# First layer norm: statistics of the second token half from eviction row sums and ScalarE squares instead of VectorE's statistics instruction

## The chip, the core and the metric

The kernel runs on one core of one Trainium2 chip. The metric is the device time of one execution in microseconds (us), here as the median of three runs. TensorE (PE) multiplies matrices and writes to PSUM; VectorE (DVE) and ScalarE (ACT) do the elementwise work; GpSimd (POOL) helps a little; SyncE (SP) issues most of the loads.

## What is computed

The reference is a trunk of two layers on 256 tokens of width 2048: a Mamba-2 mixer and then a sliding-window attention mixer, each followed by a residual and a layer norm. The change touches the norm behind the first mixer.

```python
def _layernorm(x, g, b):
    mu = jnp.mean(xf, axis=-1, keepdims=True)
    var = jnp.mean(jnp.square(xf - mu), axis=-1, keepdims=True)
    y = (xf - mu) * lax.rsqrt(var + EPS) * g + b
    return y
...
    h = _mamba2_mixer(x, ...)            # ends in  y @ w_out   (4096 x 2048)
    x = _layernorm(ALPHA * x + h, ln_g[0], ln_b[0])
    k_sh, v_sh = _shared_kv(x, kv_w, kv_b, cos, sin)   # x @ kv_w  (2048 x 512)
    h = _swa_mixer(x, k_sh, v_sh, ...)
    x = _layernorm(ALPHA * x + h, ln_g[1], ln_b[1])
```

## The kernel before

**Products in three terms.** Every float32 product of a weight matrix is made of two parts per operand, a rounded high part H and the rest L. ScalarE writes the high part of each half (1024 columns) of a 128x2048 weight unit (L143, tile wh), VectorE the low part (L144, tile wl), and TensorE runs H·H, L·H and H·L as three matmuls per 128 rows of depth. All weights come from HBM in such units, in one long list (`srcs`); `next_unit` takes the next one and starts the load and split of a unit further on.

**Residual.** The stream x lies in xr as two token halves h = 0 and 1 of 128 tokens (the partitions) by 2048 columns. The output product of the mixer is added to it group by group. An `out_unit` is 12 matmuls (L330 to L332) into one PSUM bank for one token half and one block nb of 512 columns, and one VectorE instruction that evicts it. For the mixer that is L337: xr = psum * rms + xr, where rms is a scale per token.

**The last group and the norm.** `out_last` runs the last group's units in this order: half 0 block 0, half 1 block 0, half 0 blocks 1 to 3, then `done(0)`, then half 1 blocks 1 to 3, then `done(1)`. Behind each eviction `stats` is called, which is L823: VectorE's `bn_stats` over the 512 columns just written. `done1(h)` is the norm of one half: `bn_aggr` (L827) joins the four statistics into mean and variance, ScalarE makes rs = exp(-0.5 ln(var + eps)) in two instructions (L829, L830), and then for each block c of 512 columns VectorE runs t = (x - mean) * g (L845) and xr = t * rs + b (L848), TensorE turns the four 128x128 pieces (L853), ScalarE writes the high part x1H (L858) and VectorE the low part x1L (L859).

**What comes next.** The shared K/V product reads x1H and x1L, 128 columns of the width per matmul triple (L895 to L897), four triples per weight unit, first all of half 0 and then all of half 1. So block c of x1 feeds weight unit c. A second call of `out_last` at the end of the program serves the second norm (`done2`), with L339 as eviction and the same L823 and L827.

**Order.** Up to L812 (`order.close()`) the order of each engine's instructions is the written one. Behind it the order on each engine is chosen when the program is built, from what is expected to be ready; each engine then runs its own list in that order and waits where an input is late. In the trace, for example, weight halves of the K/V product (L144), which are written behind `done1`, stand between L823 and L827.

Of the kernel before, what the change touches and what calls it, by code (L numbers as in the profile page):

```python
# [8 lines left out]
F32 = mybir.dt.float32  # L9
F32R = mybir.dt.float32r  # L10
I32 = mybir.dt.int32
AF = mybir.ActivationFunctionType
ALU = mybir.AluOpType
AX = mybir.AxisListType

P = 128
S = 256
D = 2048
KT = D // P
NG = 8  # L20
# [42 lines left out]
def trunk(ctx: ExitStack, tc: tile.TileContext, A: dict, out: bass.AP, dbg=None):  # L63
    nc = tc.nc
    PSUM = bass.MemoryType.PSUM

    def pool(name, bufs=1, side=None, space=None, stack=ctx):
        kw = {"space": space} if space is not None else {}
        return stack.enter_context(
            tc.tile_pool(name=name, bufs=bufs, side=side, reuse_waits="tile", **kw)  # L70
        )
# [9 lines left out]
    def nm(s):  # L81
        uid[0] += 1
        return f"{s}_{uid[0]}"

    def mm_tile():
        return mm_ps.tile([P, 512], F32, tag="mm", name=nm("mm"), bufs=4)

    def ax_tile():
        return ax_ps.tile([P, 512], F32, tag="ax", name=nm("ax"), bufs=4)
# [9 lines left out]
    eps_t = cst.tile([P, 1], F32, tag="eps", name="eps_t")  # L99
# [162 lines left out]
    def next_unit():  # L262
        used[0] += 1
        fill_units()
        flush()
        return units[used[0] - 1]
# [29 lines left out]
    xr = xr_all[:, : 2 * D].rearrange("p (h d) -> p h d", h=2)  # L296
# [24 lines left out]

    xH = Split("xH", 1, 0, 192)
    xL = Split("xL", 1, 64, 192)
    def out_unit(aH, aL, h, u, nb, first, rms=None):

        ps = mm_tile()
        hs = slice(h * P, (h + 1) * P)
        for k in range(4):
            ks = slice(k * 512, (k + 1) * 512)
            nc.tensor.matmul(ps[:], aH[:, k, hs], u.h[:, ks], start=k == 0, stop=False)  # L330
            nc.tensor.matmul(ps[:], aL[:, k, hs], u.h[:, ks], start=False, stop=False)  # L331
            nc.tensor.matmul(ps[:], aH[:, k, hs], u.l[:, ks], start=False, stop=k == 3)  # L332
        v = xr[:, h, nb * 512 : (nb + 1) * 512]
        if first:
            nc.vector.scalar_tensor_tensor(v, v, ALPHA, ps[:], ALU.mult, ALU.add)
        elif rms is not None:
            nc.vector.scalar_tensor_tensor(v, ps[:], rms[:, h : h + 1], v, ALU.mult, ALU.add)  # L337
        else:
            nc.vector.tensor_tensor(v, v, ps[:], ALU.add)  # L339

    def out_last(aH, aL, rms, stats, done):

        us = []
        for nb in range(4):
            us.append(next_unit())
            out_unit(aH, aL, 0, us[nb], nb, False, rms)
            stats(0, nb)
            if nb == 0:
                out_unit(aH, aL, 1, us[nb], nb, False, rms)
                stats(1, nb)  # L350
        done(0)
        for nb in range(1, 4):
            out_unit(aH, aL, 1, us[nb], nb, False, rms)
            stats(1, nb)
        done(1)

# [155 lines left out]
    gs = [G() for _ in range(NG)]  # L512
# [256 lines left out]
    for g in range(NG):  # L769
        t = 10 * g  # L770
# [51 lines left out]
    def norm_stats(st, h, nb):  # L822
        nc.vector.bn_stats(st[:, h, nb, :], xr[:, h, nb * 512 : (nb + 1) * 512])  # L823

    def norm_scale(lp, st, h):
        mv = lp.tile([P, 2], F32, tag="mv", name=nm("mv"), bufs=2)
        nc.vector.bn_aggr(mv[:], st[:, h, :, :])  # L827
        rs = lp.tile([P, 1], F32, tag="rs", name=nm("rs"), bufs=2)
        nc.scalar.activation(rs[:], mv[:, 1:2], AF.Ln, bias=eps_t[:])  # L829
        nc.scalar.activation(rs[:], rs[:], AF.Exp, scale=-0.5)  # L830
        return mv, rs

    with ExitStack() as s2:
        lp = pool("lp", stack=s2)
        gb = lp.tile([P, 2, D], F32, tag="gb", name="gb1")
        nc.gpsimd.dma_start(gb[:, 0, :], A["lng"][0].partition_broadcast(P))
        nc.gpsimd.dma_start(gb[:, 1, :], A["lnb"][0].partition_broadcast(P))
        st1 = lp.tile([P, 2, 4, 6], F32, tag="st", name="st1")

        def done1(h):  # L840
            mv, rs = norm_scale(lp, st1, h)
            for c in range(4):
                sl = slice(c * 512, (c + 1) * 512)
                t = lp.tile([P, 512], F32, tag="t", name=nm("t"), bufs=2)
                nc.vector.scalar_tensor_tensor(  # L845
                    t[:], xr[:, h, sl], mv[:, 0:1], gb[:, 0, sl], ALU.subtract, ALU.mult
                )
                nc.vector.scalar_tensor_tensor(  # L848
                    xr[:, h, sl], t[:], rs[:], gb[:, 1, sl], ALU.mult, ALU.add
                )  # L850
                ps = ax_tile()
                for k in range(4):
                    nc.tensor.transpose(  # L853
                        ps[:, k * P : (k + 1) * P], xr[:, h, c * 512 + k * P : c * 512 + (k + 1) * P], ident
                    )
                dst = (slice(None), slice(c * 4, c * 4 + 4), slice(h * P, (h + 1) * P))
                psv = ps[:].rearrange("p (k t) -> p k t", k=4)
                nc.scalar.activation(x1H[dst], psv, AF.Copy)  # L858
                nc.vector.tensor_tensor(x1L[dst], psv, x1H[dst].bitcast(F32), ALU.subtract)  # L859

        if PRE:
            tc.keep_in_program_order(nc.scalar.preload_act_table_set("natural_log_exp_and_others"))
        out_last(*gs[NG - 1].y, gs[NG - 1].rms, lambda h, nb: norm_stats(st1, h, nb), done1)
    a_stack.close()


# [37 lines left out]
    for h in range(2):  # L904
        ps = mm_tile()
# [199 lines left out]
    for what, j in B_ORDER[:-1]:  # L1105
# [5 lines left out]
        else:  # L1111
            for nb in range(4):
                u = next_unit()
# [50 lines left out]
    if PRE:  # L1164
        tc.keep_in_program_order(nc.scalar.preload_act_table_set("natural_log_exp_and_others"))
    out_last(*os_[3], None, lambda h, nb: norm_stats(st2, h, nb), done2)


# [90 lines left out]
```

## Time and profile before

| | |
|---|---|
| median of 3 runs | 986.14 us (985.79 to 987.06) |
| the profiled execution | 987.56 us, its span 985.5 us |
| granted TensorE clock | 0.998 |
| VectorE busy | 796.8 us (81%) |
| ScalarE busy | 534.2 us (54%) |
| L823 (`bn_stats`, 128x512) | 16 times, 8 of them from 643.1 to 666.9 us and 8 at the end |

The span runs from the first to the last instruction that the profiler recorded; what lies around it is 2.06 us in the profiled execution. The chain of work that ended last names, at each moment, the instruction for which the end of the program had to wait. The timeline gives each instruction's start, its duration, and in brackets the idle time of its engine just before it with what ended it. Durations of neighbouring instructions overlap a little on DVE and ACT, so the pace of a row of them is read from start to start.

### The profile page before, as it was taken

How to read it: one execution, taken by the hardware profiler on the slowest of the kernel's cores; microseconds unless marked ns; L12 is line 12 of the kernel's file. 1: busy time of each engine (PE TensorE's matmuls, PEld its weight loads, DVE VectorE, ACT ScalarE, POOL GpSimd, SP SyncE). 2: the span in 40 equal slices, each digit the busy share in tenths (PEclk: the TensorE clock that was granted, in tenths of full speed). 3: DMA queues.
4: the chain of work that ended last, by engine and by line, in shares of the span. 5: the costliest groups of instructions: out<-in, count | busy, mean ns of one | idle time of the engine just before them, and what ended most of it. 6: DMA issues, size and time to landing. Idle time of an engine off the chain costs nothing.

```text
span 985.5 us, 17642 instructions
## 1 busy us (share of the span) xinstructions
PE 977.8 (99%) x6868; PEld 879.7 (89%) x6868; DVE 796.8 (81%) x1227; ACT 534.2 (54%) x905; POOL 167.9 (17%) x223
## 2 busy tenths in 40 slices
PE   9999999999999999999999999999999999999997
PEld 7999989999998998999999999887898888778975
DVE  6879897976987896796797698999657787888786
ACT  6586847455644834743744564444356464644632
POOL 0004004005046001200400400500212222130102
PEclk9999999999999999999999999999999999999999
DMA  9587885585586666668559657756774949493942
GB/s 357 187 273 275 271 286 160 189 311 161 172 288 200 206 232 209 196 200 302 152 176 307 183 175 240 238 174 189 224 249 122 339 140 341 153 310 123 328 155 86
DMA packets 69444, 218.72 MB, mean 222 GB/s; under 512 B 8097, under 2 KB 19633, under 8 KB 68593
## 3 DMA queue, kind: packets, MB, share of 16 engines
q1 hardware_dynamic: 63936, 201.05, 62.0%
q0 software_dynamic: 5136, 16.02, 5.0%
q8 instruction: 54, 0.88, 0.4%
q10 hardware_dynamic: 288, 0.52, 0.1%
q14 instruction: 30, 0.24, 0.1%
HBM read 205.37 MB, written 12.19 MB: 221 GB/s over the span
## 4 chain that ended last, share of the span: by engine, by line
PE 96%; DVE 2%; DMA 1%; ACT 0%; issue 0%; SPq 0%
PE mm L269 18%; PE mm L270 18%; PE mm L271 18%; PE mm L330 9%; PE mm L331 9%; PE mm L332 9%; PE mm L895 3%; PE mm L896 3%; PE mm L897 3%; PE ax L619 2%; PE ax L1079 1%; PE ax L1021 1%; DMA first<-in_first 1%; DVE st L823 0%; PE ax L539 0%; DVE t L1157 0%
## 5 line engine op out<-in xcount | busy, mean ns | idle before, releaser
L144 DVE TENSOR_TENSOR wl<-wr,wh 128x1024 fp32r<-128x1024 f32 (+2 forms) x338 | 397.9, 1207 | 76.0 <-ACT wh L143 75.1
L143 ACT ACTIVATE wh<-wr 128x1024 fp32r<-128x1024 f32 (+2 forms) x338 | 328.5, 1011 | 174.1 <-PE mm L331 79.4
L269 PE MATMUL mm<-xH,wh 128*128 128x256 f32 x1280 | 355.4, 278 | 0.3 <-ACT wh L168 0.3
L270 PE MATMUL mm<-xL,wh 128*128 128x256 f32 x1280 | 354.6, 277 | 0.0
L271 PE MATMUL mm<-xH,wl 128*128 128x256 f32 x1280 | 354.3, 277 | 0.0
L269 PEld LDWEIGHTS mm<-xH,wh 128*128 128x128 f32 x1280 | 240.4, 188 | 3.7 <-ACT wh L168 2.1
L270 PEld LDWEIGHTS mm<-xL,wh 128*128 128x128 f32 x1280 | 240.5, 188 | 1.2 <-DVE xL L164 0.2
L271 PEld LDWEIGHTS mm<-xH,wl 128*128 128x128 f32 x1280 | 240.3, 188 | 0.1
L636 POOL TENSOR_TENSOR yz<-yz,z 128x256 f32<-128x256 f32 x32 | 33.3, 1060 | 436.6 <-DMA wr<-in_wa 261.1
L330 PE MATMUL mm<-wh,yH 128*128 128x512 f32 x256 | 101.2, 395 | 0.0
L331 PE MATMUL mm<-wh,yL 128*128 128x512 f32 x256 | 99.9, 390 | 0.0
L332 PE MATMUL mm<-wl,yH 128*128 128x512 f32 x256 | 99.7, 389 | 0.0
L457 DVE SCALAR_TENSOR_TENSOR cv<-mm,pc,cv 128x255 f32<-128x255 f32 x144 | 69.1, 480 | 15.2 <-ACT cv L455 11.8
L270 PE MATMUL mm<-x1L,wh 128*128 128x256 f32 x256 | 70.8, 276 | 0.0
L269 PE MATMUL mm<-x1H,wh 128*128 128x256 f32 x256 | 70.7, 276 | 0.0
L271 PE MATMUL mm<-x1H,wl 128*128 128x256 f32 x256 | 70.7, 276 | 0.0
L895 PE MATMUL mm<-wh,x1H 128*128 128x512 f32 x160 | 63.7, 398 | 0.0
L897 PE MATMUL mm<-wl,x1H 128*128 128x512 f32 x160 | 62.6, 392 | 0.2 <-DVE wl L144 0.2
L896 PE MATMUL mm<-wh,x1L 128*128 128x512 f32 x160 | 62.6, 392 | 0.2 <-DVE x1L L859 0.2
L455 ACT ACTIVATE cv<-mm,pc 128x256 f32<-128x256 f32 x48 | 26.8, 558 | 64.0 <-PE mm L271 64.0
L330 PEld LDWEIGHTS mm<-wh,yH 128*128 128x128 f32 x256 | 48.1, 188 | 10.3 <-issue 1.2
L332 PEld LDWEIGHTS mm<-wl,yH 128*128 128x128 f32 x256 | 48.1, 188 | 10.2
(220 smaller groups left out, 1371.3 us busy)
## 6 DMA issues: line engine op xcount, KB each, us to landing
wr<-in_wa SPq DMA_DIRECT2D x154, 512.0 KB, 5.4
wr<-in_wo SPq DMA_DIRECT2D x64, 512.0 KB, 5.1
wr<-in_wq SPq DMA_DIRECT2D x32, 512.0 KB, 4.9
wr<-in_wg SPq DMA_DIRECT2D x32, 512.0 KB, 5.3
wr<-in_wb SPq DMA_DIRECT2D x32, 512.0 KB, 6.2
rb<-rscr SPq DMA_DIRECT2D x16, 512.0 KB, 8.0
el<-rscr SPq DMA_DIRECT2D x16, 256.0 KB, 7.3
wr<-in_wkv SPq DMA_DIRECT2D x8, 512.0 KB, 6.4
```

Source lines behind the costliest of these rows:

```text
L143: nc.scalar.activation(h[:, sl], raw, AF.Copy)
L144: nc.vector.tensor_tensor(l[:, sl], raw, h[:, sl].bitcast(F32), ALU.subtract)
L269: nc.tensor.matmul(ps, ah, bh, start=first, stop=False)
L270: nc.tensor.matmul(ps, ah, bl, start=False, stop=False)
L271: nc.tensor.matmul(ps, al, bh, start=False, stop=last)
L330: nc.tensor.matmul(ps[:], aH[:, k, hs], u.h[:, ks], start=k == 0, stop=False)
L331: nc.tensor.matmul(ps[:], aL[:, k, hs], u.h[:, ks], start=False, stop=False)
L332: nc.tensor.matmul(ps[:], aH[:, k, hs], u.l[:, ks], start=False, stop=k == 3)
L457: nc.vector.scalar_tensor_tensor(a[:, sft:], ps[:, : S - sft], w(3 - sft), a[:, sft:], ALU.mult, ALU.add)
L895: nc.tensor.matmul(ps[:], x1H[:, kk, hs], u.h[:, ks], start=kk == 0, stop=False)
L896: nc.tensor.matmul(ps[:], x1L[:, kk, hs], u.h[:, ks], start=False, stop=False)
L897: nc.tensor.matmul(ps[:], x1H[:, kk, hs], u.l[:, ks], start=False, stop=kk == KT - 1)
```

## The change

Half 0 keeps its statistics. For half 1 of the first norm the four `bn_stats` and the `bn_aggr` go. In their place:

- the four evictions of half 1 (L337) also write the sum of each row into `acc[:, nb]`;
- after block 0, ScalarE writes nm0 = -acc[:, 0] / 512, an estimate of minus the mean that is taken from the first 512 columns; after each block it runs one 128x512 `Square` of x + nm0 whose row sum goes to `sqs[:, nb]` (its elementwise output goes to a scratch tile sq);
- behind block 3 ScalarE runs seven small instructions (`scale_sums`): minus the mean, the mean of the squares, their correction for nm0, the variance, and Ln and Exp for the scale;
- `done1(1)` adds minus the mean (`nmu`) in L845 where it subtracted the mean, and takes the scale from `rs1`.

The second norm calls `out_last` without `total`, and with no rms, so its evictions (L339) and statistics are untouched.

```diff
-            nc.vector.scalar_tensor_tensor(v, ps[:], rms[:, h : h + 1], v, ALU.mult, ALU.add)
+            nc.vector.scalar_tensor_tensor(v, ps[:], rms[:, h : h + 1], v, ALU.mult, ALU.add, accum_out=total)
...
-                out_unit(aH, aL, 1, us[nb], nb, False, rms)
+                out_unit(aH, aL, 1, us[nb], nb, False, rms, total(nb))
...
+        sums = lp.tile([P, 16], F32, tag="sums", name="sums")
+        acc, sqs, (nm0, nmu, msq, d, d2, var, rs1) = (
+            sums[:, 0:4], sums[:, 4:8], [sums[:, i : i + 1] for i in range(8, 15)]
+        )
+
+        def stats1(h, nb):
+            if h == 0:
+                norm_stats(st1, h, nb)
+                return
+            if nb == 0:
+                nc.scalar.activation(nm0, acc[:, 0:1], AF.Copy, scale=-1.0 / 512.0)
+            sq = lp.tile([P, 512], F32, tag="sq", name=nm("sq"), bufs=1)
+            nc.scalar.activation(
+                sq[:], xr[:, 1, nb * 512 : (nb + 1) * 512], AF.Square, bias=nm0, accum_out=sqs[:, nb : nb + 1]
+            )
+
+        def scale_sums():
+            junk = lp.tile([P, 8], F32, tag="junk", name="junk")
+            nc.scalar.activation(junk[:, :4], acc, AF.Copy, scale=-1.0 / D, accum_out=nmu)
+            nc.scalar.activation(junk[:, 4:], sqs, AF.Copy, scale=1.0 / D, accum_out=msq)
+            nc.scalar.activation(d, nm0, AF.Identity, scale=-1.0, bias=nmu)
+            nc.scalar.activation(d2, d, AF.Square)
+            nc.scalar.activation(var, d2, AF.Identity, scale=-1.0, bias=msq)
+            nc.scalar.activation(rs1, var, AF.Ln, bias=eps_t[:])
+            nc.scalar.activation(rs1, rs1, AF.Exp, scale=-0.5)
+
         def done1(h):
-            mv, rs = norm_scale(lp, st1, h)
+            if h:
+                scale_sums()
+                shift, sop, rs = nmu, ALU.add, rs1
+            else:
+                mv, rs = norm_scale(lp, st1, h)
+                shift, sop = mv[:, 0:1], ALU.subtract
...
-                    t[:], xr[:, h, sl], mv[:, 0:1], gb[:, 0, sl], ALU.subtract, ALU.mult
+                    t[:], xr[:, h, sl], shift, gb[:, 0, sl], sop, ALU.mult
...
-        out_last(*gs[NG - 1].y, gs[NG - 1].rms, lambda h, nb: norm_stats(st1, h, nb), done1)
+        out_last(*gs[NG - 1].y, gs[NG - 1].rms, stats1, done1, lambda nb: acc[:, nb : nb + 1])
```

## What was predicted before the change was timed

> **What bounds the kernel now.** I read the page first: its span (985.5 us), the busy times, and the chain of work that ended last.
>
> ```profile
> PE 977.8 (99%) x6868; PEld 879.7 (89%) x6868; DVE 796.8 (81%) x1227; ACT 534.2 (54%) x905; POOL 167.9 (17%) x223
> ...
> PE 96%; DVE 2%; DMA 1%; ACT 0%; issue 0%; SPq 0%
> ```
>
> TensorE sets the end. The change takes nothing from TensorE, so it can only pay where TensorE waits. All that it can win lies in the 2% of the chain that is VectorE. So I asked for the chain of waits from 659 to 675 us, where the first norm is. Its columns are start, duration, and what ran.
>
> ```profile
> 659.48 0.69 DVE x1L L859
> ...
> 664.01 1.19 DVE st L823 x2
> 665.20 0.65 DVE xr L337
> 665.85 1.13 DVE wl L144
> 666.98 0.60 DVE st L823
> 667.59 1.12 DVE wl L144
> 668.71 0.17 DVE mv L827
> 668.88 1.08 DVE wl L144
> 669.96 0.72 DVE t L845 x2
> 671.20 0.76 DVE xr L848
> ...
> 673.39 0.70 DVE x1L L859
> ...
> 674.14 0.50 PE mm L896
> ```
>
> From 659.48 to 671.96 us the chain is VectorE's queue, one instruction behind the other: it is working off a backlog. Three statistics of half 1 stand in it (664.01 twice, 666.98) and the `bn_aggr` (668.71). At 674.14 us TensorE gets the first low part of half 1 and the chain is TensorE's again. How much TensorE lost there is read from its own timeline: start, duration, line, and in brackets its idle time.
>
> ```profile
> 666.48 0.39 PE L896 MATMUL mm<-wh,x1L 128*128 128x512 f32 x1
> 667.04 0.50 PE L897 MATMUL mm<-wl,x1H 128*128 128x512 f32 x1 [0.17 <-DVE wl L144]
> 667.38 0.39 PE L895 MATMUL mm<-wh,x1H 128*128 128x512 f32 x1
> ...
> 668.30 0.40 PE L896 MATMUL mm<-wh,x1L 128*128 128x512 f32 x1
> 668.76 0.50 PE L897 MATMUL mm<-wl,x1H 128*128 128x512 f32 x1
> ...
> 671.39 0.39 PE L896 MATMUL mm<-wh,x1L 128*128 128x512 f32 x1
> 672.09 1.29 PE L853 MATMUL ax<-cc,xr 128*128 128x128 f32 x8 [0.31 <-DVE xr L848]
> 673.41 0.51 PE L895 MATMUL mm<-wh,x1H 128*128 128x512 f32 x1
> 674.14 0.50 PE L896 MATMUL mm<-wh,x1L 128*128 128x512 f32 x1 [0.22 <-DVE x1L L859]
> ...
> 675.40 0.39 PE L895 MATMUL mm<-wh,x1H 128*128 128x512 f32 x1
> 675.63 0.60 PE L853 MATMUL ax<-cc,xr 128*128 128x128 f32 x4
> 675.98 0.49 PE L896 MATMUL mm<-wh,x1L 128*128 128x512 f32 x1
> ```
>
> The bracketed idle times understate the loss, since a matmul's recorded 0.39 us overlaps the next; starts tell more. In steady running the next matmul starts 0.23 us later (675.40 to 675.63), and four transposes take 0.35 us (675.63 to 675.98). Against that: 666.48 to 667.04 loses 0.33, and the step after it (0.34) another 0.11; 668.30 to 668.76 loses 0.23, and I put the same 0.11 behind it, 0.34 together; 671.39 to 672.09 loses 0.47; the eight transposes to 673.41 take 1.32 and not 0.70, so 0.62; 673.41 to 674.14 loses 0.50, with 0.10 behind it. Sum: 0.44 + 0.34 + 0.47 + 0.62 + 0.60 = about **2.4 us**. This is the ceiling in this stage, 0.25% of the time. The first two losses (0.78) are waits for a weight half (wl), the rest (1.7) waits for the norm of half 1; all have VectorE's backlog behind them.
>
> **What the change removes.** Half 1's four L823 and one L827. The first L823 of half 1 stands at about 643.7 us, in the pair that starts at 643.1, ahead of the backlog: its 0.6 us is worth nothing. In the backlog go 1.19 + 0.60 + 0.17 = **1.96 us** of VectorE's queue.
>
> **What it adds on VectorE.** Four evictions with a row sum, of which three (blocks 1 to 3) are in the backlog. No VectorE instruction with a row sum is in this trace. The nearest rows are ScalarE's exponentials with a row sum, where the sum is read out by an instruction of its own, and VectorE's smallest instructions.
>
> ```profile
> 860.19 0.19 ACT L1044 ACTIVATION_READ_ACCUMULATOR p<-p,sm 128x1 f32 x1
> 860.28 0.39 ACT L1044 ACTIVATE p<-p,sm 128x128 f32<-128x128 f32 x1
> ...
> L676 DVE SCALAR_TENSOR_TENSOR r<-r 128x2 f32<-128x2 f32 x24 | 3.9, 161 | 0.8
> L337 DVE SCALAR_TENSOR_TENSOR xr<-mm,r,xr 128x512 f32<-128x512 f32 x64 | 45.6, 742 | 3.5 <-PE mm L332 3.4
> L848 DVE SCALAR_TENSOR_TENSOR xr<-t,rs,gb 128x512 f32<-128x512 f32 x8 | 5.8, 743 | 0.0
> L548 DVE TENSOR_TENSOR e<-e,cbm 128x1536 f32<-128x1536 f32 x16 | 27.6, 1754 | 0.2
> L1049 DVE TENSOR_TENSOR p<-p,sm 128x1024 f32<-128x1024 f32 x8 | 9.7, 1215 | 0.0
> ```
>
> The read-out moves ScalarE's next start by 0.09 us (860.19 to 860.28). A VectorE instruction on two elements lasts 0.161. I take 0.10 per eviction, the nearest being the read-out itself: 3 x 0.10 = 0.30 us. Bounds: 0 (the sum is free) and 0.16 per eviction (0.48 together). A larger cost, a slower pass of the eviction itself, is a rival below. The page "Vector Engine (DVE) Microarchitecture Reference" of the Trainium skill speaks against the change here: § Points that are easy to get wrong says that this kind of instruction runs at half rate when both sources are wide SBUF tensors, as no port is left for the accumulator. This trace shows no such loss without a sum: L848, with both sources in SBUF, takes 743 ns and L337, with one in PSUM, 742 ns; with a sum no run here shows it yet. By that rule, were it to hold for the eviction too, the sum would be that of the fourth rival.
>
> Net on VectorE's queue: 1.96 - 0.30 = **1.66 us** less ahead of 674 us.
>
> **What it adds on ScalarE.** ScalarE was idle for 6 us in the stretch in question, up to 668.92.
>
> ```profile
> 632.92 1.28 ACT L862 ACT_TABLE_LOAD   x1
> ...
> 652.43 0.29 ACT L829 ACTIVATE rs<-mv,eps_t 128x1 f32<-128x1 f32 x1 [7.18 <-DVE mv L827]
> ...
> 661.70 1.21 ACT L858 ACTIVATE x1H<-ax 128x512 fp32r<-128x512 f32 x2
> 668.92 0.29 ACT L829 ACTIVATE rs<-mv,eps_t 128x1 f32<-128x1 f32 x1 [6.01 <-DVE mv L827]
> 669.24 0.20 ACT L830 ACTIVATE rs<-rs 128x1 f32<-128x1 f32 x1
> ...
> L1160 ACT ACTIVATE t<-t,rs 128x512 f32<-128x512 f32 x4 | 2.8, 721 | 1.3 <-DVE t L1157 1.3
> ```
>
> A `Square` of 512 columns with a pointer operand I price as L1160, 0.72 us, plus 0.10 for the read-out: 0.82. Those of blocks 1 and 2 can run from about 662.9 on, when the two L858 are done, into 6 us of idle time; they cost nothing. The one of block 0 and the nm0 copy run near 644 us, ahead of the 7.18 us of idle time before 652.43; nothing is queued behind them there but one weight cast.
>
> Block 3 starts the chain that matters. Its eviction moves from 665.20 to 665.20 - 1.19 + 0.20 = 664.2, and ends with its sum at about 664.95. Then Square, to 665.8. Then seven small instructions, each needing the one before or nearly so; a step takes 0.32 (668.92 to 669.24), two of them with 0.10 for a read-out: 7 x 0.32 + 0.20 = 2.44. So minus the mean is there at about 666.2 and the scale at **668.2 us**.
>
> Is that in time? In VectorE's queue L845 would come at 669.96 - 1.66 = 668.3 and the first L848 at 671.20 - 1.66 = 669.5. The chain is ready 1.3 us before L848 wants it, because the three weight halves (1.13 + 1.12 + 1.08) stand in front. If that cover were gone, L848 would wait, and the weight halves behind it. The new wait thus has a margin of 1.3 us against an estimated chain of 3.3 us. No DMA is issued, moved or passed by the change; the SP and POOL queues keep their lists.
>
> **What is late next.** With 1.66 us less, the first low part of half 1 (L859) starts at 671.7 and TensorE's L896 at 674.14 - 1.66 = 672.5. Without the two waits for weight halves TensorE reaches that point at 671.39 - 0.78 + 0.23 + 0.70 + 0.23, about 671.8. So 0.7 us of the stall is left, and TensorE is 1.66 us ahead of before. Does it keep this? Behind 690 us the waits of TensorE are a single row, at the very end:
>
> ```profile
> PE ax L1146 <- ACT dg L1136: 0.9, 1, 0.9
> ```
>
> Nothing is waited for in between, so weights and casts, which follow TensorE's consumption, have room for it to be 1.7 us earlier.
>
> **Sum.** Span 985.5 - 1.66 = 983.8; the profiled execution had 987.56 - 985.5 = 2.06 around it, so 985.9. The profiled one was 1.42 above the median shown, so as a median 986.14 - 1.66 = **984.5 us**. With both bounds of the read-out the gain is 1.5 to 2.0.
>
> **The rivals.**
>
> *The whole stall goes* (983.8). Behind L812 the order is chosen anew. If the weight halves fill the wait for ScalarE and the blocks of the norm go ahead of the third half, TensorE never starves and all 2.4 us are won. For it: the chain is ready by 668.2, and the remaining stall of 0.7 us is smaller than one weight half. Against it: VectorE has no gap to give, and the third half is itself needed by about 669.5. 983.4 to 984.1.
>
> *The norm waits a little for ScalarE* (985.4). The margin of 1.3 us goes if the new order assumes a shorter chain than the hardware needs, or puts Squares in front of the two L858. A table switch belongs here: the table load at 632.92 takes 1.28 us, and one in the chain would use up the margin. The Trainium skill's page "ScalarE: Activation LUTs", § Table sets: the hidden batching unit, says that cheap functions are in every set but does not name Square among its examples; no row before shows one. The gain is then 0.3 to 1.2 us.
>
> *The weight halves are held up* (987.6, slower). VectorE runs its list in order. If L845 and L848 of half 1 are put ahead of the first weight half, L845 stands waiting for ScalarE until 666.2, two L845 take it to 667.5, L848 waits until 668.2 and two of them take 1.4; then 1.13 for the weight half: 670.7. TensorE needs that half at 666.48 + 0.23 = 666.7, and so loses 4.0 us where it lost 2.4: 1.6 slower. If all four blocks go first (six more instructions of 0.66 in place of the two L848), it is 673.3 and 4.2 slower, 990.3. The point from which it decides: the first half must be done by 666.7 + 2.4 = 669.1. For it: the norm is written ahead of these loads. Against it: in the chain above a weight half stands in each gap between dependent steps (behind 665.20, 666.98 and 668.71), so such gaps have been filled.
>
> *The row sum doesn't relieve VectorE* (986.0). If an eviction with a sum streamed at half rate, it would cost as much as 512 more elements: 1754 - 1215 = 0.54 us (L548 against L1049). Three of them are 1.6 us, and the gain is gone. So it is, too, if the evictions wait for ScalarE's writes to the neighbouring columns of `sums`. Against the latter: TensorE reads the first half of a weight unit at 667.04 while VectorE writes the second from 667.59, so waits go by region.
>
> **How the numbers follow.** Forecast 0.44 (984.1 to 985.0), whole stall 0.25, small wait 0.16, held-up halves 0.09, no relief 0.06. The range takes in all but the held-up halves and the edges: 983.4 to 986.4. A measurement of this kernel can tell about 0.2%, or 2.0 us, from no change, so most of the forecast's cases count as the same: faster 0.28 (the whole stall, and the edge of the forecast), slower 0.07 (most of the held-up halves), same 0.65.
>
> **What will show it.** L823 falls from 16 to 12 and L827 from 4 to 3. The chain of waits near 665 us has no L823 and a short VectorE read-out; evictions stay at 0.74 us (else the fourth rival). ScalarE's scale is ready before VectorE's first L848 of half 1, with no bracketed wait on ScalarE there (else the second or third). TensorE's gap before the transposes of half 1 falls from 0.47 to near nothing, and the low part of half 1 comes about 1.7 us earlier. The prediction is wrong if TensorE waits longer for a wl than before, or if it gains here and new waits appear behind 690 us.

## The result, and the profile after

| | before | changed |
|---|---|---|
| median of 19 runs each, us | 986.76 (985.04 to 988.39) | 984.98 (983.31 to 985.66) |
| ratio of the two, 95% interval | | 0.998 [0.9974, 0.9987] |
| span of the profiled execution, us | 985.5 | 983.5 |

The changed kernel is 1.78 us faster by the medians. The interval of the ratio, times 986.76, makes that 1.3 to 2.6 us: a small gain, but not none. The forecast was a gain of 1.66 us.

Lines behind the change have new numbers: L845 is now L876, L848 is L879, the transposes L853 are L884, the high part L858 is L889, the low part L859 is L890, and the K/V matmuls L895 to L897 are L926 to L928. New are L850 (nm0), L852 (Square) and L858 to L864 (the seven small steps). First the page of the changed kernel, its busy times and the chain that ended last:

```profile
PE 976.9 (99%) x6868; PEld 880.0 (89%) x6868; DVE 794.3 (81%) x1226; ACT 538.8 (55%) x921; POOL 168.0 (17%) x223
...
PE 98%; DVE 1%; ACT 0%; issue 0%
```

VectorE gave up 2.5 us (796.8 to 794.3), ScalarE took on 4.6 (534.2 to 538.8), and TensorE's share of the chain rose from 96 to 98%. Of these two points only VectorE's (2% before, 1% now) is the change's; the other is the 1% of DMA in the chain before, one of the program's first loads (`first`). The groups of instructions by line, of the changed kernel (busy us and mean ns of one behind the first bar, idle time behind the second):

```profile
L337 DVE SCALAR_TENSOR_TENSOR xr<-mm,r,xr 128x512 f32<-128x512 f32 x64 | 45.6, 742 | 3.3 <-PE mm L332 3.2
L823 DVE BATCH_NORM_STATS2 st<-xr 128x6 f32<-128x512 f32 x12 | 8.3, 694 | 0.4
```

The statistics fell from 16 to 12, and the evictions stay at 742 ns. That is a mean of 64, of which four have a row sum; the three of these in the stage take 0.74 us each.

**Where in the program the gain lies.** The stage is measured from the first K/V matmul to the first transposed key, both on TensorE. Start, duration and line from TensorE's timeline, before and then changed:

```profile
659.81 0.39 PE L895 MATMUL mm<-wh,x1H 128*128 128x512 f32 x1
...
697.69 1.03 PE L922 MATMUL ax<-cc,kd 128*128 128x128 f32 x8
```

```profile
659.47 0.39 PE L926 MATMUL mm<-wh,x1H 128*128 128x512 f32 x1
...
696.00 1.03 PE L953 MATMUL ax<-cc,kd 128*128 128x128 f32 x8
```

The stretch fell from 37.88 to 36.53 us: 1.35 us of the 2.0 between the two spans. The rest is not the change's. The start at 659 us is 0.34 earlier already; 0.33 of that is there within the program's first 25 us. And about 900 us the unchanged kernel's profile loses 0.32 us among attention matmuls, which a kernel that keeps all statistics (the first experiment) doesn't lose either, though it gains nothing in this stage.

**How the stage runs now.** VectorE's timeline of the changed kernel, from the eviction of half 1's block 2 on:

```profile
661.74 0.74 DVE L337 SCALAR_TENSOR_TENSOR xr<-mm,r,xr 128x512 f32<-128x512 f32 x1
662.41 0.08 DVE L337 DVE_READ_ACCUMULATOR xr<-mm,r,xr 128x1 f32 x1
662.41 0.68 DVE L890 TENSOR_TENSOR x1L<-ax,x1H 128x512 fp32r<-128x512 f32 x1
663.01 0.74 DVE L337 SCALAR_TENSOR_TENSOR xr<-mm,r,xr 128x512 f32<-128x512 f32 x1
...
664.28 1.21 DVE L144 TENSOR_TENSOR wl<-wr,wh 128x1024 fp32r<-128x1024 f32 x1
665.41 1.40 DVE L876 SCALAR_TENSOR_TENSOR t<-xr,sums,gb 128x512 f32<-128x512 f32 x2
666.74 1.41 DVE L879 SCALAR_TENSOR_TENSOR xr<-t,sums,gb 128x512 f32<-128x512 f32 x2
...
668.96 1.32 DVE L890 TENSOR_TENSOR x1L<-ax,x1H 128x512 fp32r<-128x512 f32 x2 [0.15 <-ACT x1H L889]
...
671.52 1.22 DVE L144 TENSOR_TENSOR wl<-wr,wh 128x1024 fp32r<-128x1024 f32 x1
```

Two things are to be seen. The read-out of the row sum is recorded at the very moment at which the next instruction starts (662.41), so it takes no place in the queue: 0.67 us lie from an eviction's start to the next start. And the order is another. Before, three weight halves stood between the last eviction and the norm of half 1; now one does (664.28), and the second follows only at 671.52. So the first low part of half 1 starts at 668.96 where it started at 673.39: 4.4 us earlier (4.1 behind the stage's own start), not 1.7.

ScalarE's timeline of the changed kernel, behind the last eviction:

```profile
663.89 0.73 ACT L852 ACTIVATE sq<-xr,sums 128x512 f32<-128x512 f32 x1
...
664.61 0.19 ACT L858 ACTIVATE junk<-sums 128x4 f32<-128x4 f32 x1
664.99 0.28 ACT L860 ACTIVATE sums<-sums 128x1 f32<-128x1 f32 x1
665.30 0.20 ACT L861 ACTIVATE sums<-sums 128x1 f32<-128x1 f32 x1
...
666.19 0.20 ACT L864 ACTIVATE sums<-sums 128x1 f32<-128x1 f32 x1
```

The scale is there at 666.39 (666.19 and 0.20), 0.35 us before VectorE's first L879 at 666.74, which shows no bracketed wait. No table load stands in the chain: both kernels have four in the whole program, on the same lines but for the shift.

TensorE's timeline of the changed kernel, at the norm of half 1:

```profile
667.47 0.39 PE L927 MATMUL mm<-wh,x1L 128*128 128x512 f32 x1
667.70 1.22 PE L884 MATMUL ax<-cc,xr 128*128 128x128 f32 x8
668.98 0.50 PE L926 MATMUL mm<-wh,x1H 128*128 128x512 f32 x1
669.71 0.50 PE L927 MATMUL mm<-wh,x1L 128*128 128x512 f32 x1 [0.22 <-DVE x1L L890]
670.04 0.40 PE L928 MATMUL mm<-wl,x1H 128*128 128x512 f32 x1
```

Read from starts as in the prediction: 667.47 to 667.70 is the steady 0.23, nothing lost (before 0.47). The eight transposes take 1.28 instead of 0.70: 0.58. From 668.98 to 669.71 are 0.73 instead of 0.23: 0.50. Then 0.33: 0.10. Together 1.2 us lost, against 2.4 before. Both waits for a weight half are gone. TensorE's list was changed with VectorE's: 32 K/V matmuls stand ahead of these transposes, where 44 stood. The chain of work that ended last shows what the remaining loss consists of:

```profile
667.86 0.45 PE ax L884 x4
...
668.33 0.61 ACT x1H L889
...
668.96 0.70 DVE x1L L890
...
669.71 0.50 PE mm L927
```

It is no longer a backlog of VectorE's. It is the way from a block's transposes over the high part and the low part to the matmul, 1.85 us (667.86 to 669.71), in which TensorE's list holds too little else. In the chain of the kernel before, some 12 us of VectorE stood at this place. Behind the stage, TensorE has in the view of waits of the changed kernel only the one at the very end that was there before:

```profile
PE ax L1177 <- ACT dg L1167: 0.9, 1, 0.9
```

So the gain is kept to the end.

### The profile page after: what moved, and what is told of

Same layout as the page of the kernel before. It is cut to its first block, busy times and chain, and to the rows that moved or that the text cites. A ratio compares the mean times of both kernels' runs of the same rounds, so it can differ in the third digit from the quotient of the medians.

```text
span 983.5 us, 17660 instructions
## 1 busy us (share of the span) xinstructions
PE 976.9 (99%) x6868; PEld 880.0 (89%) x6868; DVE 794.3 (81%) x1226; ACT 538.8 (55%) x921; POOL 168.0 (17%) x223
## 4 chain that ended last, share of the span: by engine, by line
PE 98%; DVE 1%; ACT 0%; issue 0%
PE mm L269 18%; PE mm L270 18%; PE mm L271 18%; PE mm L330 9%; PE mm L331 9%; PE mm L332 9%; PE mm L926 4%; PE mm L927 4%; PE mm L928 4%; PE ax L619 2%; PE ax L1110 1%; PE ax L1052 1%; PE ax L198 1%; PE ax L539 0%; DVE t L1188 0%; PE ax L1177 0%
## 5 line engine op out<-in xcount | busy, mean ns | idle before, releaser
L926 PE MATMUL mm<-wh,x1H 128*128 128x512 f32 x160 | 63.6, 397 | 0.1
L928 PE MATMUL mm<-wl,x1H 128*128 128x512 f32 x160 | 62.5, 390 | 0.0
```

Of the source, the lines that this page charges most:

```text
L926: nc.tensor.matmul(ps[:], x1H[:, kk, hs], u.h[:, ks], start=kk == 0, stop=False)
L928: nc.tensor.matmul(ps[:], x1H[:, kk, hs], u.l[:, ks], start=False, stop=kk == KT - 1)
```

## The experiments

The theory, called A, is that of the prediction: VectorE's time ahead of half 1's low parts is what TensorE pays for, so the statistics' time is the gain, and ScalarE's chain costs nothing since VectorE has other work meanwhile. The rivals put the gain or a loss on the row sums, on ScalarE's chain or on the new order; each expectation says what they give for that kernel. Every run was timed in five rounds with the unchanged kernel on the same chip. "Stretch" is the stage as above, 37.88 before and 36.53 changed, from one profile each; it is the finer measure, since the medians of the same kernel before moved from 986.66 to 987.24 between chips.

| | median, us | kernel before, us | ratio, 95% interval | stretch, us |
|---|---|---|---|---|
| row sums alone | 987.06 | 986.66 | 1.0002 [0.9993, 1.001] | 37.97 |
| statistics back | 987.09 | 986.66 | 1.0008 [0.9998, 1.0017] | 38.27 |
| no chain | 985.49 | 986.66 | 0.9997 [0.9988, 1.0006] | 36.73 |
| longer chain | 985.47 | 986.66 | 0.9989 [0.998, 0.9998] | 36.67 |
| half between | 984.65 | 987.24 | 0.9978 [0.9969, 0.9988] | 36.06 |
| GpSimd adds | 986.04 | 987.24 | 0.9989 [0.9978, 1.0001] | 37.11 |
| both of these | 985.40 | 987.24 | 0.9985 [0.9975, 0.9995] | 37.10 |
| second norm too | 986.59 | 986.71 | 1.0 [0.9989, 1.001] | 36.55 |
| changed again | 984.95 | 986.71 | 0.9984 [0.9974, 0.9995] | 36.50 |
| half between again | 984.72 | 986.71 | 0.9979 [0.9968, 0.9989] | 36.09 |

### Row sums alone

The kernel before with the row sum on the evictions of half 1, which nobody reads.

```diff
-            nc.vector.scalar_tensor_tensor(v, ps[:], rms[:, h : h + 1], v, ALU.mult, ALU.add)
+            nc.vector.scalar_tensor_tensor(v, ps[:], rms[:, h : h + 1], v, ALU.mult, ALU.add, accum_out=total)
...
-        out_last(*gs[NG - 1].y, gs[NG - 1].rms, lambda h, nb: norm_stats(st1, h, nb), done1)
+        out_last(*gs[NG - 1].y, gs[NG - 1].rms, lambda h, nb: norm_stats(st1, h, nb), done1, lambda nb: acc[:, nb : nb + 1])
```

> The kernel before with row sums added to the four evictions of half 1; nobody reads them, the statistics stay. In the profile after, the read-out stands beside the next eviction without moving it (661.07, 661.74, 662.41). Theory A (a row sum is free on VectorE): the same time as before, 986.8 within 0.5, the evictions 0.74 us each with 0.67 us from start to start, and the stretch from the first K/V matmul to the first transposed key 37.9 us as before. Theory B (0.10 us each, as the prediction took it): 0.3 us more in that stretch, 38.2.

VectorE's timeline of this kernel:

```profile
661.95 0.08 DVE L337 DVE_READ_ACCUMULATOR xr<-mm,r,xr 128x1 f32 x1
661.95 0.74 DVE L337 SCALAR_TENSOR_TENSOR xr<-mm,r,xr 128x512 f32<-128x512 f32 x1
...
673.31 1.35 DVE L861 TENSOR_TENSOR x1L<-ax,x1H 128x512 fp32r<-128x512 f32 x2
```

The order is that of before, the stretch 37.97 against 37.88, the ratio 1.0002. The read-out starts with the next instruction and delays nothing. The low part comes at 673.31, 13.63 us behind the first K/V matmul, where it came 13.58 behind it (673.39 less 659.81). The row sums are free and bring nothing by themselves.

### Statistics back

The changed kernel with the four `bn_stats` of half 1 in it again, unread.

```diff
             if h == 0:
                 norm_stats(st1, h, nb)
                 return
+            norm_stats(st1, h, nb)
```

> The changed kernel with VectorE's four statistics of half 1 put back; nobody reads them, mean and scale still come from ScalarE. VectorE's list then has one weight half ahead of the norm of half 1, as in the changed kernel, but three statistics more. Theory A (what counts is VectorE's time ahead of the first low part of half 1): that comes 1.8 us later than in the changed kernel, the gain is gone, 986.8 to 987.3, stretch 38.0 to 38.5 us. Theory B (what counts is the new order, one weight half ahead of the norm where three stood): 985.0 to 985.4, stretch 36.5 to 36.9.

The stretch is 38.27, 1.75 us more than the changed kernel's 36.53. Three of the four statistics stand in the backlog, 0.60 each from start to start: 1.8. TensorE's timeline of this kernel shows where they go:

```profile
668.77 0.39 PE L928 MATMUL mm<-wh,x1L 128*128 128x512 f32 x1
670.16 1.29 PE L885 MATMUL ax<-cc,xr 128*128 128x128 f32 x8 [1.00 <-DVE xr L880]
```

The transposes come 1.39 us behind the last matmul and not 0.23, so 1.16 is lost to a wait that the changed kernel doesn't have. Another 0.5 goes at a wait for a weight half, and the 1.2 behind the transposes stays. That is about 2.9 in all, by the same reading. ScalarE's chain and the order with one weight half ahead are still those of the changed kernel, so neither of them is the source of the gain: the statistics' time is. More than that: the stretch is 0.39 longer than before the change (37.88), so beside the same statistics the new order with ScalarE's part costs some 0.4, and the gain of 1.35 is what is left of 1.75. (This kernel also has a wait of 1.1 us in the attention, for `sg`; it may be in the median, and is not in the stretch.)

### No chain

The Squares and the seven steps are left out, and half 1 is normed with the mean and scale of half 0; so its output isn't the reference's.

```diff
-            if nb == 0:
-                nc.scalar.activation(nm0, acc[:, 0:1], AF.Copy, scale=-1.0 / 512.0)
...
+            return
...
-                scale_sums()
-                shift, sop, rs = nmu, ALU.add, rs1
+                mv, rs = half0
```

> The changed kernel without ScalarE's Squares and small instructions: half 1 is scaled with the mean and the scale of half 0, so its own statistics are left out. Theory A (ScalarE's chain is hidden behind VectorE's backlog): no faster than the changed kernel, 984.6 to 985.6, although the norm may start right behind the last eviction; what is then ahead of the weight halves TensorE has to wait for. Theory B (the chain is on the path): faster by the 1.1 us that lie between the last eviction's end and the first use of the mean, 983.9, stretch 35.4 us.

VectorE's timeline, and then TensorE's, of this kernel:

```profile
663.14 1.41 DVE L877 SCALAR_TENSOR_TENSOR t<-xr,mv,gb 128x512 f32<-128x512 f32 x2
...
666.66 1.36 DVE L891 TENSOR_TENSOR x1L<-ax,x1H 128x512 fp32r<-128x512 f32 x2
...
669.26 1.22 DVE L144 TENSOR_TENSOR wl<-wr,wh 128x1024 fp32r<-128x1024 f32 x1
```

```profile
665.37 1.29 PE L885 MATMUL ax<-cc,xr 128*128 128x128 f32 x8
...
667.41 0.50 PE L928 MATMUL mm<-wh,x1L 128*128 128x512 f32 x1 [0.23 <-DVE x1L L891]
```

With nothing to wait for, the norm of half 1 goes right behind the last eviction, ahead of every weight half. The low part comes still earlier, at 666.66, and yet the stretch is 36.73, not shorter than 36.53: TensorE's list also goes to half 1 sooner and loses the same way from transposes to low part (665.37 to 667.41 for the first matmul on a low part). A chain of no length at all wins nothing, so the real one is hidden. And the low part's time alone doesn't set the end. That rests on the trace: in time this kernel isn't told from the one before (its interval holds 1.0, and its executions go from 984.25 to 987.90, of which the fastest was profiled).

### Longer chain

Four more dependent steps on minus the mean.

```diff
             nc.scalar.activation(junk[:, :4], acc, AF.Copy, scale=-1.0 / D, accum_out=nmu)
+            for _ in range(4):
+                nc.scalar.activation(nmu, nmu, AF.Copy)
```

> The changed kernel with four more small ScalarE instructions in the chain, each needing the one before, ahead of the mean's first use; a step of this kind took 0.2 to 0.3 us, so the mean and the scale come about 1.1 us later. Theory A (the wait is covered, since a second weight half takes its place on VectorE, 1.13 us that TensorE needs anyway): within 0.4 us of the changed kernel, 984.6 to 985.4, stretch 36.2 to 36.9. Theory B (the chain is on the path): 1.1 us slower, 986.1, stretch 37.6.

VectorE's timeline of this kernel:

```profile
664.77 2.35 DVE L144 TENSOR_TENSOR wl<-wr,wh 128x1024 fp32r<-128x1024 f32 x2
667.03 1.41 DVE L878 SCALAR_TENSOR_TENSOR t<-xr,sums,gb 128x512 f32<-128x512 f32 x2
```

The four steps make the chain some 0.9 us longer. Two weight halves instead of one were put ahead of the norm, VectorE doesn't wait, and the stretch is 36.67, 0.14 longer. Repeats of the changed kernel and of the next one below differ by 0.03, so that may be a small cost, but not the 0.9 of the steps: the order absorbs most of a longer chain.

### Half between

If the remaining 1.2 us is latency that TensorE has nothing to fill with, one more split weight half, put between the blocks of the norm, should give it matmuls.

```diff
                 nc.scalar.activation(x1H[dst], psv, AF.Copy)
                 nc.vector.tensor_tensor(x1L[dst], psv, x1H[dst].bitcast(F32), ALU.subtract)
+                if h and c == 0:
+                    ahead[0] = 3
+                    fill_units()
+                    ahead[0] = 2
```

> The changed kernel with the third K/V unit's load and split written between block 0 and block 1 of half 1's norm, so that VectorE's list has two weight halves ahead of block 0's end where it had one. In the changed kernel TensorE still loses 1.2 us while block 0 of half 1 is turned, split high and split low, since it has run out of half 0's matmuls. Theory A (it lacks work that a weight half would give: six matmuls, 1.36 us, for 1.13 us of VectorE): the loss falls to 0.5 to 0.9 us, stretch from the first K/V matmul to the first transposed key 35.8 to 36.3 us, 984.4 to 984.8. Theory B (VectorE's total is what counts and the order doesn't): 36.5 as in the changed kernel.

VectorE's timeline, and then TensorE's, of this kernel:

```profile
663.98 1.22 DVE L144 TENSOR_TENSOR wl<-wr,wh 128x1024 fp32r<-128x1024 f32 x1
665.11 0.75 DVE L876 SCALAR_TENSOR_TENSOR t<-xr,sums,gb 128x512 f32<-128x512 f32 x1
665.77 1.22 DVE L144 TENSOR_TENSOR wl<-wr,wh 128x1024 fp32r<-128x1024 f32 x1
```

```profile
668.11 0.60 PE L884 MATMUL ax<-cc,xr 128*128 128x128 f32 x4
668.47 0.49 PE L932 MATMUL mm<-wl,x1H 128*128 128x512 f32 x1
...
669.40 0.50 PE L930 MATMUL mm<-wh,x1H 128*128 128x512 f32 x1
669.79 0.63 PE L884 MATMUL ax<-cc,xr 128*128 128x128 f32 x4
670.30 0.50 PE L931 MATMUL mm<-wh,x1L 128*128 128x512 f32 x1
```

The transposes of the first block (four now, not eight) take their steady 0.36 us and TensorE goes on with matmuls of half 0. No matmul in the stage has a bracketed wait, but by starts some 0.6 us are still lost around the second block's transposes: 0.38 instead of 0.23 up to 669.40, 0.39 instead of 0.23 up to 669.79, 0.51 instead of 0.35 up to 670.30, and 0.1 behind that. TensorE's weight load (PEld), which comes ahead of each matmul, shows what the first of these is, a wait for the high part:

```profile
669.40 0.19 PEld L930 LDWEIGHTS mm<-wh,x1H 128*128 128x128 f32 x1 [0.41 <-ACT x1H L889]
```

The stretch is 36.06 and in the repeat 36.09, 0.4 under the changed kernel. In the medians that isn't resolved: 984.72 against 984.95 on the same chip, with intervals that overlap for the most part. By the traces it is the best here; by the times it isn't told from the changed kernel.

### GpSimd adds, and both

VectorE is relieved further: for the last two blocks of half 0, ScalarE multiplies by the scale and GpSimd adds b.

```diff
+                if h == 0 and c >= 2:
+                    nc.scalar.activation(t[:], t[:], AF.Copy, scale=rs[:])
+                    nc.gpsimd.tensor_tensor(xr[:, h, sl], t[:], gb[:, 1, sl], ALU.add)
+                else:
```

> The changed kernel with the second step of blocks 2 and 3 of half 0 taken off VectorE: ScalarE scales by rs and GpSimd adds b, as the second norm of this kernel does for its half 0. That takes 2 x 0.66 = 1.3 us out of VectorE's backlog in front of half 1's evictions. Theory A (VectorE's time there is still the bound): the 1.2 us that TensorE still loses fall to 0.3 or less, stretch 35.4 to 35.8 us, 984.0 to 984.3. Theory B (what is left is the latency of turning and splitting block 0, whatever VectorE has to do): 36.5, 985.0.

TensorE's timeline of this kernel, at half 0's transposes:

```profile
659.20 0.40 PE L930 MATMUL mm<-wh,x1H 128*128 128x512 f32 x1
660.17 0.65 PE L888 MATMUL ax<-cc,xr 128*128 128x128 f32 x4 [0.57 <-POOL xr L881]
661.40 0.66 PE L888 MATMUL ax<-cc,xr 128*128 128x128 f32 x4 [0.58 <-POOL xr L881]
```

This missed what either theory expected. The stall at half 1 is gone, but TensorE now waits twice at half 0's transposes: 0.97 instead of 0.23 from 659.20, and 1.23 instead of 0.36 to the second four, 1.6 us together. GpSimd takes 1.26 us for each add (two in 2.51), VectorE's L879 took 0.66 from start to start, and TensorE's list has those transposes ahead of the matmuls that could run. Less work for VectorE is no gain when the engine in its place is later with the same tile.

The two edits together:

> Both edits together. Theory A: TensorE's loss in the stretch is gone, 35.3 to 35.6 us, 983.8 to 984.2; no more than with the GpSimd step alone if that one leaves nothing. Theory B: 36.5.

The same two waits, 1.2 us by the view of waits, and a stretch of 37.1. The half between doesn't help where the list stands at an earlier transpose.

### Second norm too

The same exchange at the end of the program, where no other work stands behind the evictions: L339 becomes an instruction with a row sum, and half 1's statistics go to ScalarE.

```diff
+            nc.vector.scalar_tensor_tensor(v, v, 1.0, ps[:], ALU.mult, ALU.add, accum_out=total)
...
+        nc.scalar.activation(
+            sq[:], xr[:, 1, nb * 512 : (nb + 1) * 512], AF.Square, bias=nm2, accum_out=sqs2[:, nb : nb + 1]
+        )
...
+            scale_sums2()
...
-    out_last(*os_[3], None, lambda h, nb: norm_stats(st2, h, nb), done2)
+    out_last(*os_[3], None, stats2, done2, lambda nb: acc2[:, nb : nb + 1])
```

> The changed kernel with the same exchange made in the second norm's half 1 too: row sums from the evictions, ScalarE's Squares and the seven small instructions in place of four statistics and the aggregate. There nothing follows that VectorE or TensorE could do meanwhile, and the last eviction waits for TensorE's last matmul, so it does not come earlier. From its end to the scale it took 0.72 + 0.30 + 0.55 = 1.6 us in the kernel before (statistics, aggregate, Ln and Exp) and ScalarE's chain took 2.6 us in the first norm of the changed kernel. Theory A (the exchange pays only where VectorE has a backlog and the chain has cover): the last transposed product (TensorE's matmuls with the diagonal of the scale) starts 1.0 us later behind the last eviction, and the kernel is 1.0 us slower than the changed one, 986.0. Theory B (fewer VectorE instructions pay wherever they stand): three statistics and the aggregate, 2.3 us, are gone behind the first of these evictions, and it is 1 us or more faster, 984.0.

The timeline at the end of the changed kernel, and then of this one, from the last eviction to the product with the scale:

```profile
973.01 0.69 DVE L339 TENSOR_TENSOR xr<-xr,mm 128x512 f32<-128x512 f32 x1
...
975.78 3.61 PE L1177 MATMUL ax<-t,dg 128*128 128x512 f32 x4 [0.89 <-ACT dg L1167]
```

```profile
973.44 0.69 DVE L339 SCALAR_TENSOR_TENSOR xr<-xr,mm 128x512 f32<-128x512 f32 x1 [1.41 <-PE mm L332]
...
977.21 3.78 PE L1206 MATMUL ax<-t,dg 128*128 128x512 f32 x4 [1.90 <-ACT dg L1196]
```

From the start of the last eviction to that product are 2.77 us with VectorE's statistics and 3.77 with ScalarE's chain: 1.0 us longer, and TensorE waits for it (1.90 instead of 0.89). By the medians on one chip it is 986.59 against 984.95 for the changed kernel, 1.6 longer, of which this place shows 1.0. The exchange as such is slower here. It pays in the first norm because VectorE is behind there and has other work in the meantime.

### The repeats

> The changed kernel once more, on the same chip as the next one: 985.0 within 0.5, stretch from the first K/V matmul to the first transposed key 36.5 us.

> The kernel with a weight half between block 0 and block 1 once more, to set it beside the changed kernel on one chip. If its stretch of 36.0 us against 36.5 is the whole difference, it is 0.5 us faster than the changed kernel, within what five rounds can tell from none; if the later order has changed to the worse somewhere, less.

The changed kernel again: 984.95, a stretch of 36.50 (first 36.53), and the same waits. The half between again: 984.72 and 36.09 (first 36.06).

## Why the prediction was right, and where its steps were off

**What bounds the kernel, and the ceiling**: right. The lost time of TensorE was the place of the gain. The five terms of that sum make 2.47 and not 2.4; 1.18 is lost now, so 1.29 of it went, and the stretch is 1.35 shorter. Nothing was given back behind 690 us.

**What the change removes**: right. Putting the statistics back makes the stretch 1.75 longer, against 1.79 for three statistics in the prediction's rows (1.19 and 0.60).

**What it adds on VectorE**: 0.10 per eviction was too much. It is nothing, the lower of the two bounds. The net relief was 1.96 us and not 1.66. Evictions stay at 742 ns, so the fourth rival falls. That row bears on the rule of the Trainium skill weighed there ("Vector Engine (DVE) Microarchitecture Reference", § Points that are easy to get wrong): it speaks of two wide sources in SBUF, and an eviction has one of its two in PSUM. No run here had a row sum with both in SBUF, so the rule is neither borne out nor refuted.

**What it adds on ScalarE**: the chain was over-priced. From the end of the last eviction (663.75) to the scale (666.39) are 2.64 us, not 3.3. A step that needs the one right before it takes 0.24 to 0.33 (0.31 from 664.99 to 665.30), near the 0.32 assumed; the first two steps with their read-outs take 0.38 together (664.61 to 664.99). Square ran without a table load, as the page "ScalarE: Activation LUTs" of the Trainium skill, § Table sets: the hidden batching unit, would have it if Square belongs to its cheap functions.

**The margin**: right in outcome, wrong in its working. It was 0.35 us and not 1.3, because the norm didn't stay behind three weight halves. The cover that the prediction named had mostly gone, and the chain still hid, behind one weight half and two L876.

**What is late next** is the step that failed. The prediction kept the order and moved everything by 1.66: low part at 671.7, a stall of 0.7 left. The order was chosen anew; the low part came at 668.96, and the stall left is 1.2, of another kind. TensorE's list was changed along with VectorE's, so an earlier low part met earlier transposes. That the sum came out near (1.35 in the trace, 1.78 by the medians, 1.66 forecast) rests on the removed time being real, not on this step: of the 1.96 us that VectorE was relieved of, the new order let TensorE keep 1.35, 0.3 less than forecast. That the medians lie nearer to the forecast than the trace does is luck, since their interval reaches from 1.3 to 2.6. What decides how much of the relief a new order turns into gain wasn't worked out here beyond these kernels.

**The rivals.** *The whole stall goes* had the order nearly right (blocks ahead of the third half, even of the second) and its conclusion wrong: TensorE starves from latency. The half between comes within 0.6 of it. *The norm waits a little* didn't happen; the longer chain shows that the order makes room. *The weight halves are held up* was mispriced: without the chain the norm does stand ahead of all weight halves, and where the rival's working gave a loss of 1.6 to 4.2 us (986.14 and 1.6 make 987.7, not 987.6), the stretch was 36.73, 1.15 shorter than before. In that kernel the norm had no ScalarE to wait for, so that part of the rival's price wasn't run. The rest of its error is the one above, a list of TensorE taken as fixed. *The row sum doesn't relieve VectorE* fell with the first experiment.

## What to carry to other kernels

Moving work from one engine to another paid here where the first was behind and the second's result wasn't awaited, and not elsewhere: the same exchange gained 1.35 us where VectorE had a backlog and cost 1.0 at the end of the program, where it was the chain itself. Where the order of the instructions is chosen anew at each build, shifting the old timeline doesn't give the size of a gain, because the other engines' lists move too. Here the time removed (1.96 us) was more than came of it (1.35), and a build with the old work in the new order (statistics back) showed where the rest went. Once a backlog is gone, look at what latency is left and whether the waiting engine's list has work to put into it.

## What the runs showed of the hardware that was not expected

A VectorE row sum is read out by an instruction of 0.08 us that is recorded at the same start as the next one, and the pace from start to start is 0.67 us, where it was 0.66 without the sum. On ScalarE small instructions (128x1 and 128x4) that don't need the one right before them start 0.09 to 0.10 us apart, and dependent ones 0.23 to 0.33. GpSimd's 128x512 add takes 1.26 us, nearly twice the 0.66 in which VectorE scales and adds.
